# Where sums and scalings run in a hybrid decoder block: row normalisation on VectorE from PSUM, kv latent weights split earlier, gate weights scaled by ScalarE, output splits spread

## The chip, the core and the metric

The kernel runs on one core of a Trainium2 chip. The core has a matrix engine (TensorE, PE in the profile, with its weight loads as PEld), a vector engine (VectorE, DVE), a scalar engine (ScalarE, ACT), a general engine (GpSimd, POOL) and a queue for data transfers (SyncE, SP). They run in parallel, each through its own list of instructions in order, and wait for one another by semaphores. The metric is the device time of one execution in microseconds (us); of several runs the median counts.

## The reference

One decoder block on 1024 rows (S) of width 1024 (D), all in float32. What is computed:

```
h  = rmsnorm(x, mix_norm_g)
p  = h @ w_in    # q 512 | k 128 | v 128 | q latent 384 | kv latent 256 | rope key 32 | gate a 1024 | gate b 1024
A  = sliding-window attention (window 128, 8 heads on 2 kv heads, sinks, rope) of q, k, v
B  = latent attention: q from rmsnorm(q latent) @ w_uq; k, v from rmsnorm(kv latent) @ w_ukv; causal, 8 heads
y  = sigmoid(gate a) * (A @ w_o_swa) + sigmoid(gate b) * (B @ w_o_mla)
x  = x + y @ w_out
h  = rmsnorm(x, ffn_norm_g)
x  = x + (silu(h @ w_gate) * (h @ w_up)) @ w_down        # width 2816
out = rmsnorm(x, final_norm_g)
```

rmsnorm(x, g) is x times 1/sqrt(mean(x*x) + 1e-6) per row, times g per column.

## The kernel before

**Precision.** Every large product is made of three matmuls. Both factors are split into a rounded part hi and a remainder lo (function split, lines 159 to 161: ACT copies src into hi with rounding, L160, and DVE subtracts hi from src into lo, L161). mm3 (L163 to 169) then adds hi*hi, hi*lo and lo*hi in PSUM; the three lines L167, L168 and L169 are PE's rows in the profile. Weights whose rows carry the norm's gain are split by split_g: ACT scales and rounds (L215), DVE multiplies and subtracts in one instruction (L216), one piece of 128 rows at a time.

**Stages.** They follow each other on PE:

1. The q pass (about 20 to 85 us). For each of eight blocks b of 128 rows, kvq(b) makes k, v and the head half of q, q_first(b) the rest of q, from the normalised and transposed block xt[b]. square(b) sums the squares on ACT, POOL makes 1/rms and writes it on the diagonal of a 128x128 tile dg (L398; a ring of four tiles). spread(b) multiplies a matrix of ones by that tile on PE (L402), so that 1/rms stands in every partition, in PSUM (rb). normalize(b) multiplies xt[b] by it: for b < 5 (RAW) ACT copies rb to SBUF (L407) and POOL multiplies, for b = 5 to 7 DVE multiplies straight from PSUM (both L409). to_quad(b) splits xt[b] into hh and hl, h_out(b) stores it. rope_q and rope_kvq apply rope on DVE (L370 to 377) and store through SP, k_transposes and k_split bring the keys into khd.
2. The ql pass (85 to 121.5): the q latents. set_of_h(c) loads pairs of stored blocks of h back (load_set, two U buffers each) and makes sums and differences of them (t1, t2, t3, t4) for the seven-product scheme below. latent_end(b) reads the latent from PSUM. The two units of kl weights are fetched and split by st.get at b = 6 and 7.
3. The kl pass (121.5 to 156.6): the kv latents of eight blocks (lines 951 to 979), 24 matmuls each. Into it are put the first window-attention steps (sw_qT(0), sw_scores(0)), the preparation of the first gate weights (gates.prep_to, gates.mix(0)) and kv_out(b), the scaling and store of each latent.
4. The gates (156.6 to 345): class Seven (L697) makes each column j of the gates by a scheme of seven half-size products (numbered 1 to 7 and run in ORDER = 1, 6, 2, 7, 5, 4, 3). mix(j) makes three sums of weight halves on POOL (L622, L625 are the helpers sub and add), prep splits the weights of a product three products ahead, and scale_gate (L802 to 809) multiplies them by the gain, column 0 on DVE, the others on POOL, four instructions per half. Column 0 has an order written out (head). Sixteen steps of the window attention are put between the products: sw_q load, sw_qT transposes, sw_scores (DVE's max nm at L897, ACT's exponential at L905), sw_pT, sw_pv.
5. The MLA attention (345 to 548), with the stored window outputs loaded and split for the output projection near its end (load_oa, split_oa).
6. The output projections (548 to 750), then the FFN up to 1388: again class Seven for w_gate and w_up (columns of both are products g and u, prepared four ahead), then the down projection.

**What sets the order.** PE and SP run in program order up to line 1559. ACT, DVE and POOL run in program order up to the end of the kl pass (by_hand, L485 to L979); after that a planner orders these three. U is a pool of 21 buffers, V one of 17; a load or a result waits until its buffer is free. PSUM has pool ps1 (P1) and a pool of the phase (PX).

## Time and profile before

| | |
|---|---|
| median of three runs | 1392.3 us (1391.87 to 1393.46) |
| the profiled execution | 1390.31 us |
| its span, first to last instruction | 1388.5 us |
| PE busy | 1347.6 us, 97% |
| DVE, ACT, POOL busy | 922.9, 621.1, 600.9 us |
| mean granted PE clock | 0.994 of full speed |
| read from and written to HBM | 141.24 MB, 59.77 MB |

A row of the timeline reads: start in us, length in us (the summed length for several in one row, ending in x2, x4), engine, line, operation, result <- operands by their names in the program, shape, number. Brackets give the engine's idle time just before and what ended it: "[1.95 <-DVE wl L216]" is an engine that stood still for 1.95 us until the tile wl was written by DVE in line 216. A row of the groups reads: line, engine, operation, number | busy us, mean ns of one | idle time before and its releasers. A row of the waits: who waited for whom, us in total, times, the longest. PEclk is the clock that PE was granted, 1.00 being full.

### The profile page before, as it was taken

What the parts mean: (1) busy time and instruction counts of PE and PEld (TensorE: products, weight loads), DVE (VectorE), ACT (ScalarE), POOL (GpSimd) and SP (SyncE); (2) the same over time, 40 slices, a digit from 0 to 9 for tenths busy, and PEclk for the clock granted to TensorE, in tenths of its full rate; (3) what the DMA queues carried; (4) which work ended last, traced back from release to release, by engine and by line L of the source; (5) the groups of instructions that cost most, each with busy time, mean ns of one, the idle gap of its engine ahead of it and who ended that gap; (6) DMA issues with size and microseconds to landing.
All of it is one profiled execution on the core that took longest, in us unless ns stands there. A gap on an engine that the chain in (4) does not pass through costs nothing.

```text
span 1388.5 us, 18957 instructions
## 1 busy us (share of the span) xinstructions
PE 1347.6 (97%) x6600; PEld 1124.8 (81%) x6600; DVE 922.9 (66%) x1481; ACT 621.1 (45%) x1248; POOL 600.9 (43%) x643
## 2 busy tenths in 40 slices
PE   9897999999999999999999899999999999999997
PEld 6797887888888887888887688888888888888886
DVE  6868578778767788476449856655566565664762
ACT  7433455654566777553226322223233223644353
POOL 2414575766145565120021556686555652022421
PEclk9998999999999999999999999999999999999999
DMA  9454223323400010473154244454444324997504
GB/s 360 149 178 148 74 80 115 107 95 118 163 1 12 13 61 17 160 269 117 46 213 143 83 168 175 167 199 150 174 160 162 140 101 171 363 387 268 167 5 147
DMA packets 78095, 202.25 MB, mean 146 GB/s; under 512 B 8752, under 2 KB 15408, under 8 KB 78000
## 3 DMA queue, kind: packets, MB, share of 16 engines
q1 hardware_dynamic: 77856, 201.04, 40.5%
q8 instruction: 52, 0.85, 0.2%
q14 instruction: 43, 0.35, 0.1%
q10 hardware_dynamic: 144, 0.00, 0.0%
HBM read 141.24 MB, written 59.77 MB: 145 GB/s over the span
## 4 chain that ended last, share of the span: by engine, by line
PE 77%; DVE 7%; issue 4%; POOL 3%; ACT 3%; DMA 1%; SPq 0%; POOLq 0%; ACTq 0%; DVEq 0%
PE fa L169 7%; PE fa L167 7%; PE fa L168 7%; PE fb L167 5%; PE fb L168 5%; PE fb L169 5%; PE fd L169 5%; PE fd L167 5%; PE fd L168 5%; PE xo L167 2%; PE xo L169 2%; PE xo L168 2%; PE pTb L1148 2%; PE oA L167 1%; PE oA L169 1%
## 5 line engine op out<-in xcount | busy, mean ns | idle before, releaser
L161 DVE TENSOR_TENSOR wl<-wr,wl 128x512 fp32r<-128x512 f32 x150 | 153.0, 1043 | 78.7 <-ACT wl L160 78.4
L161 DVE TENSOR_TENSOR lrv<-lr,lrv 128x1024 fp32r<-128x1024 f32 x77 | 105.1, 1396 | 50.3 <-ACT lrv L160 49.2
L160 ACT CAST lrv<-lr 128x1024 fp32r<-128x1024 f32 x77 | 80.1, 1052 | 96.1 <-PE fd L169 55.8
L168 PE MATMUL fd<-lrv 128*128 128x512 f32 x308 | 119.9, 389 | 0.0
L169 PE MATMUL fd<-lrv 128*128 128x512 f32 x308 | 119.8, 389 | 0.0
L167 PE MATMUL fd<-lrv 128*128 128x512 f32 x308 | 119.8, 389 | 0.0
L622 POOL TENSOR_TENSOR wr<-wr,sm 128x512 f32<-128x512 f32 x30 | 43.6, 1452 | 122.5 <-DVE wl L161 122.5
L160 ACT CAST wl<-wr 128x512 fp32r<-128x512 f32 x150 | 87.0, 622 | 1.1 <-DVE t4l L161 0.8
L293 POOL TENSOR_SCALAR ms<-ss 128x1 f32<-128x1 f32 x32 | 8.1, 254 | 176.7 <-ACT xn L1520 111.2
L161 DVE TENSOR_TENSOR wl<-sm,wl 128x512 fp32r<-128x512 f32 x60 | 49.6, 853 | 37.3 <-ACT wl L160 37.1
L1133 POOL TENSOR_TENSOR denb<-denb,neg_one 128x1 f32<-128x1 f32 x64 | 36.5, 570 | 72.9 <-ACT p L1132 69.5
L168 PEld LDWEIGHTS fd<-lrv 128*128 128x128 f32 x308 | 57.8, 188 | 12.4 <-DVE lrv L161 0.3
L169 PEld LDWEIGHTS fd<-lrv 128*128 128x128 f32 x308 | 57.8, 188 | 12.1
L167 PEld LDWEIGHTS fd<-lrv 128*128 128x128 f32 x308 | 57.8, 188 | 11.8
L1132 ACT ACTIVATE p<-scb,nmb 128x384 f32<-128x384 f32 (+3 forms) x64 | 47.6, 744 | 35.5 <-DVE nmb L1131 34.1
L161 DVE TENSOR_TENSOR ptl<-pTb,pth 128x512 fp32r<-128x512 f32 (+2 forms) x96 | 50.1, 549 | 13.0 <-ACT pth L160 12.7
L1131 DVE CUSTOM_DVE_ANT_0 scb<-scb,mask 128x384 f32<-128x384 f32 (+3 forms) x64 | 48.4, 757 | 13.4 <-PE scb L1123 13.1
L1412 ACT ACTIVATE act<-sm 128x512 f32<-128x512 f32 x11 | 7.0, 634 | 110.6 <-DVE sm L625 110.6
L905 ACT ACTIVATE pe<-sc,nm 128x256 f32<-128x256 f32 (+1 forms) x64 | 28.8, 458 | 55.5 <-DVE nm L897 55.5
L625 POOL TENSOR_TENSOR sm<-wr,wr 128x512 f32<-128x512 f32 x30 | 40.9, 1363 | 28.4 <-DVE t4l L161 15.2
L167 PE MATMUL fb<-t3h,wl 128*128 128x512 f32 x120 | 48.0, 400 | 5.0 <-DVE pu L625 3.8
L1134 POOL TENSOR_SCALAR p<-p,denb 128x384 f32<-128x384 f32 (+3 forms) x64 | 49.1, 768 | 6.3
(347 smaller groups left out, 4370.3 us busy)
## 6 DMA issues: line engine op xcount, KB each, us to landing
lr<-la_d SPq DMA_DIRECT2D x77, 256.0 KB, 5.4
wr<-in_w_gate_dram SPq DMA_DIRECT2D x22, 512.0 KB, 3.8
wr<-in_w_up_dram SPq DMA_DIRECT2D x22, 512.0 KB, 4.9
wd<-in_w_down_dram SPq DMA_DIRECT2D x22, 512.0 KB, 7.0
rb_d<-wd SPq DMA_DIRECT2D x22, 512.0 KB, 2.6
la_d<-sd SPq DMA_DIRECT2D x22, 512.0 KB, 5.4
lr<-rb_d SPq DMA_DIRECT2D x44, 256.0 KB, 5.4
lr<-in_w_down_dram SPq DMA_DIRECT2D x33, 256.0 KB, 5.3
```

Of the source, the lines that this page charges most:

```text
L160: nc.scalar.copy(hi, src)
L161: (eng or nc.vector).tensor_tensor(lo, src, hi.bitcast(F32), op=ALU.subtract)
L167: nc.tensor.matmul(ps, ah, bh, start=first and i == 0, stop=False, skip_group_check=go_on)
L168: nc.tensor.matmul(ps, ah, bl, start=False, stop=False, skip_group_check=go_on)
L169: nc.tensor.matmul(ps, al, bh, start=False, stop=last and i == n - 1, skip_group_check=go_on)
L622: eng.tensor_tensor(out, a, b, op=ALU.subtract)
L625: eng.tensor_tensor(out, a, b, op=ALU.add)
L905: nc.scalar.activation(pe[:, h, c0:], scs[h // 2][:, h % 2, c0:], AF.Exp, scale=SC_A, bias=nm[:, h:h + 1], accum_out=den[:, h:h + 1])
L1131: nc.vector.tensor_tensor_reduce(s_, s_, m_, 1.0, -NEG, op0=ALU.add, op1=ALU.min, accum_out=nm)
L1132: nc.scalar.activation(p_, s_, AF.Exp, scale=-1.0, bias=nm, accum_out=den)
L1133: nc.gpsimd.tensor_tensor(den, den, neg_one[:, 0:1], op=ALU.pow)
L1134: nc.gpsimd.tensor_scalar(p[:, 0:w], p[:, 0:w], den, 0.0, op0=ALU.mult, op1=ALU.add)
```

## The change

It moves work between engines and along the programs of the engines, and keeps the matmuls; column 0 of the gates runs its products 2 and 6 in the other order.

- normalize always multiplies on DVE from PSUM; ACT's copy of rb and POOL's multiply go. The ring of dg has seven tiles. k_split makes both ACT copies before both subtractions. In the hand-written order of the q pass to_quad(2), to_quad(3), to_quad(6), to_quad(4), square(7) and normalize(7) come earlier, in front of rope and key steps.
- The kl weights are split at b = 0 and 2 of the ql pass. set_of_h runs latent_end ahead of its splits and POOL's subtractions in two halves. sw_q(0) is loaded at b = 6. sw_qT takes the phase's PSUM pool.
- In the kl pass mix(0) runs on DVE at i = 3, prep_to(2) at i = 4, gate part (1, 0) is loaded at i = 4; kv_out runs two blocks behind up to i = 4.
- The gates' head is gone. For j >= 1 ACT scales the gate weights, in pieces given by scale_at (product, half, first piece, count). mix runs at product 5 and no longer at 7; the sums on POOL are made in halves of 128x256.
- After the last prod_v the weights wv and wkv2 are dropped, and the window outputs are loaded and split in eight single steps of the attention.
- In the FFN mix(1) runs on DVE after the loop, with prep_to(14) ahead of it.

```diff
--- before.py
+++ after.py
...
     dgt = U("dg", F32, (P, 8, P))
-    ones, dg, rbs = dgt[:, 7], dgt[:, 0:4], dgt[:, 4:7]
+    ones, dg = dgt[:, 7], dgt[:, 0:7]
...
         rstd_of(sums.pop(b), D, r)
-        nc.gpsimd.tensor_scalar(dg[:, b % 4], ident, r, 0.0, op0=ALU.mult, op1=ALU.add)
+        nc.gpsimd.tensor_scalar(dg[:, b % 7], ident, r, 0.0, op0=ALU.mult, op1=ALU.add)
...
         rb[b] = P1("rb", (P, P))
-        nc.tensor.matmul(rb[b], ones, dg[:, b % 4], start=True, stop=True)
+        nc.tensor.matmul(rb[b], ones, dg[:, b % 7], start=True, stop=True)
...
     def normalize(b):
-        r, eng = rb.pop(b), nc.vector
-        if b < RAW:
-            nc.scalar.copy(rbs[:, b % 3], r)
-            r, eng = rbs[:, b % 3], nc.gpsimd
-        eng.tensor_tensor(xt[b], xt[b], r.unsqueeze(1).to_broadcast([P, NK, P]), op=ALU.mult)
+        nc.vector.tensor_tensor(xt[b], xt[b], rb.pop(b).unsqueeze(1).to_broadcast([P, NK, P]), op=ALU.mult)
...
         for g in range(NG):
-            split(khd[g][0][:, blk(b)], khd[g][1][:, blk(b)], pt[:, g])
+            nc.scalar.copy(khd[g][0][:, blk(b)], pt[:, g])
+        for g in range(NG):
+            sub(khd[g][1][:, blk(b)], pt[:, g], khd[g][0][:, blk(b)].bitcast(F32), nc.vector)
...
     h_out(5)
+    to_quad(2)
     rope_q(1)
-    to_quad(2)
...
     st.load_to(st.index[("ql", 0)])
+    square(7)
+    to_quad(6)
     rope_kvq(5)
-    to_quad(6)
-    square(7)
...
     h_out(6)
+    to_quad(3)
     rope_q(2)
+    normalize(7)
     k_split(4)
-    normalize(7)
-    to_quad(3)
...
     k_twice(6)
+    to_quad(4)
...
     rope_q(3)
-    to_quad(4)
...
         sub(r[:, 0], t[:, 0], r[:, 0], nc.vector)
-        sub(t[:, 0], t[:, 1], t[:, 0], nc.gpsimd)
-        split_h("t1", c, r[:, 0])
+        for k in range(0, 4, 2):
+            k = slice(k, k + 2)
+            sub(t[:, 0, k], t[:, 1, k], t[:, 0, k], nc.gpsimd)
...
         sub(t[:, 1], t[:, 1], r[:, 0], nc.vector)
-        split_h("t3", c, t[:, 0])
-        sub(t4_raw[-1][:, c % 2], r[:, 1], t[:, 1], nc.gpsimd)
-        split_h("t2", c, t[:, 1])
+        for i, src in ((1, r[:, 0]), (3, t[:, 0]), (2, t[:, 1])):
+            split_h(f"t{i}", c, src)
+        for k in range(0, 4, 2):
+            k = slice(k, k + 2)
+            sub(t4_raw[-1][:, c % 2, k], r[:, 1, k], t[:, 1, k], nc.gpsimd)
...
-        def __init__(self, pairs, ms, load, done, ahead, load_at, mix_at, head=(), at=None, scale=None):
+        def __init__(self, pairs, ms, load, done, ahead, load_at, mix_at, head=(), at=None, scale=None, scale_at=(), piece=4):
...
                 self.at.setdefault((j, load_at[1]), []).append(("load", j + 1, 1))
+                for q, *args in scale_at:
+                    self.at.setdefault((j, q), []).append(("scale", j + 1, *args))
...
             self.scale = scale
+            self.piece = piece
...
+        def scale_part(self, j, kh, k=0, n=4):
+            for k in range(k, k + n):
+                if self.scale is not None and (j, kh, k) not in self.scaled:
+                    self.scaled.add((j, kh, k))
+                    self.scale(j, kh, k, self.raws[(j, kh)])
...
             self.load_part(j, kh)
-            if self.scale is not None and (j, kh) not in self.scaled:
-                self.scaled.add((j, kh))
-                self.scale(j, kh, self.raws[(j, kh)])
+            self.scale_part(j, kh)
...
-        def mix(self, j):
+        def mix(self, j, eng=None):
...
                 s = self.sums[(j, m)] = U("sm", F32, (P, 2, 4, P))
-                add(s[:, 0], a21, a22, nc.gpsimd)
-                sub(s[:, 1], s[:, 0], a11, nc.gpsimd)
-                sub(a21, a11, a21, nc.gpsimd)
+                eng_, n = (eng, 4) if eng is not None else (nc.gpsimd, self.piece)
+                for k in range(0, 4, n):
+                    k = slice(k, k + n)
+                    add(s[:, 0, k], a21[:, k], a22[:, k], eng_)
+                    sub(s[:, 1, k], s[:, 0, k], a11[:, k], eng_)
+                    sub(a21[:, k], a11[:, k], a21[:, k], eng_)
...
             if q == 7:
-                a12 = self.part(j, m, 1, 0)
-                sub(a12, a12, self.sums[(j, m)][:, 1], nc.gpsimd)
+                a12, s1 = self.part(j, m, 1, 0), self.sums[(j, m)][:, 1]
+                for k in range(0, 4, self.piece):
+                    k = slice(k, k + self.piece)
+                    sub(a12[:, k], a12[:, k], s1[:, k], nc.gpsimd)
...
                 for what, *args in self.at.get((j, q), ()):
-                    (self.load_part if what == "load" else self.mix)(*args)
+                    {"load": self.load_part, "mix": self.mix, "scale": self.scale_part}[what](*args)
...
-    def scale_gate(j, kh, raw):
+    def scale_gate(j, kh, k, raw):
         t = raw["g"]
-        for k in range(4):
-            g = gT[:, 4 * kh + k:4 * kh + k + 1]
-            if j == 0:
-                nc.vector.tensor_scalar(t[:, k], t[:, k], g, None, op0=ALU.mult)
-            else:
-                nc.gpsimd.tensor_scalar(t[:, k], t[:, k], g, 0.0, op0=ALU.mult, op1=ALU.add)
+        g = gT[:, 4 * kh + k:4 * kh + k + 1]
+        if j == 0:
+            nc.vector.tensor_scalar(t[:, k], t[:, k], g, None, op0=ALU.mult)
+        else:
+            nc.scalar.activation(t[:, k], t[:, k], AF.Copy, scale=g)
...
-    gates = Seven(NK, "g", load_gate, gate_done, 3, (1, 6), 7, [(0, q) for q in (1, 2, 6, 7, 5, 4, 3)],
-                  {(0, 1): [("load", 1, 0)], (0, 6): [("load", 1, 1)], (0, 7): [("mix", 1)]}, scale_gate)
+    gates = Seven(NK, "g", load_gate, gate_done, 3, (1, 6), 5, scale=scale_gate, scale_at=[(2, 0, 0, 2), (7, 0, 2, 2), (7, 1, 0, 2), (5, 1, 2, 2)], piece=2)
...
             latent_end(b - 1)
-        if b >= 6:
-            wkl.append(st.get(("kl", b - 6)))
+        if b == 6:
+            sw_q(0)
+        if b in (0, 2):
+            wkl.append(st.get(("kl", b // 2)))
...
         ql_ps[b] = (t, ps, rstd_of(ss, QL))
-    sw_q(0)
...
         qn = d.pop("qn")
-        ptq = P1("qT", (P, 2, P))
+        ptq = PX("qT", (P, 2, P))
...
         if i == 3:
-            gates.prep_to(2)
+            gates.mix(0, nc.vector)
...
             sw_scores(0)
+            gates.prep_to(2)
...
             t4_of_h(i - 4)
-        if i == 5:
-            gates.mix(0)
         scaled.append((t, r, b))
-        if i >= 1:
+        if i == 4:
+            gates.load_part(1, 0)
+        while len(scaled) > (2 if i < 5 else 1):
             kv_out(*scaled.pop(0))
-    kv_out(*scaled.pop(0))
+    while scaled:
+        kv_out(*scaled.pop(0))
     gates.prep_to(3)
+    gates.load_part(1, 0)
...
         prod_v(b)
+    del wv
+    wkv2.pop()
...
-    def load_oa(sh):
-        for g in range(2):
-            oa_raw[(g, sh)] = U("oar", F32, (P, 2, 512))
-            nc.sync.dma_start(oa_raw[(g, sh)], oa_d[2 * g + sh])
-    def split_oa(g, sh):
-        raw = oa_raw.pop((g, sh))
-        hi, lo = halves_of((P, 2, 512), True)
-        for c in range(2):
-            split(hi[:, c], lo[:, c], raw[:, c])
-            oaT[(2 * g + c, sh)] = (hi[:, c], lo[:, c])
+    def load_oa(g, sh):
+        oa_raw[(g, sh)] = U("oar", F32, (P, 2, 512)), halves_of((P, 2, 512), True)
+        nc.sync.dma_start(oa_raw[(g, sh)][0], oa_d[2 * g + sh])
+    def split_oa(g, sh, c):
+        raw, (hi, lo) = oa_raw[(g, sh)] if c == 0 else oa_raw.pop((g, sh))
+        split(hi[:, c], lo[:, c], raw[:, c])
+        oaT[(2 * g + c, sh)] = (hi[:, c], lo[:, c])
...
     wo = {}
+    OA_LOAD = {-26: (0, 0), -22: (1, 0), -14: (0, 1), -10: (1, 1)}
+    OA_SPLIT = {-22: (0, 0, 0), -20: (0, 0, 1), -18: (1, 0, 0), -16: (1, 0, 1),
+                -10: (0, 1, 0), -8: (0, 1, 1), -6: (1, 1, 0), -4: (1, 1, 1)}
...
         e = t - (NT - 8)
-        if e == -13:
-            load_oa(0)
-        if e == -10:
-            load_oa(1)
-        if e in (-10, -9, -7, -6):
-            i = (-10, -9, -7, -6).index(e)
-            split_oa(i % 2, i // 2)
+        if e in OA_LOAD:
+            load_oa(*OA_LOAD[e])
+        if e in OA_SPLIT:
+            split_oa(*OA_SPLIT[e])
...
             ffn.prep_to(12)
-        if i == 5:
-            ffn.mix(1)
...
             late_split(i - 2)
+    ffn.prep_to(14)
+    ffn.mix(1, nc.vector)
...
```

More of the change, by code (lines that the diff above doesn't have):

```diff
@@ L169, in mm3, with sub, add @@
             nc.tensor.matmul(ps, al, bh, start=False, stop=last and i == n - 1, skip_group_check=go_on)
+    def sub(out, a, b, eng):
+        eng.tensor_tensor(out, a, b, op=ALU.subtract)
+    def add(out, a, b, eng):
+        eng.tensor_tensor(out, a, b, op=ALU.add)
     def blk(b, n=1):
@@ L618, in hybrid_block_kernel @@
     del wqa
-    def sub(out, a, b, eng):
-        eng.tensor_tensor(out, a, b, op=ALU.subtract)
-    def add(out, a, b, eng):
-        eng.tensor_tensor(out, a, b, op=ALU.add)
     hq = {}
```

## The prediction

> **What bounds the kernel now.** I read the page's shares first, then busy time by stretch, then each row of PE's timeline that begins with an idle time, then the VectorE (DVE), ScalarE (ACT) and GpSimd (POOL) rows under it.
>
> ```profile
> span 1388.5 us, 18957 instructions
> PE 1347.6 (97%) x6600; PEld 1124.8 (81%) x6600; DVE 922.9 (66%) x1481; ACT 621.1 (45%) x1248; POOL 600.9 (43%) x643
> ```
>
> PE is the bound: 1388.5 - 1347.6 = 40.9 us is all its idle time. The matmuls stay the same in number and shape, so only this idle time, and matmuls run at a lowered clock, can be won. By stretch (time, length, PE, its weight loads, DVE, ACT, POOL, granted PE clock, DMA share, GB/s):
>
> ```profile
> 20.00:85.00 65.00, 60.95 (x364) 52.49 (x363) 54.72 (x115) 31.36 (x80) 22.15 (x23) 1.00 0.56 195
> 85.00:121.50 36.50, 36.50 (x196) 36.12 (x195) 23.00 (x53) 10.93 (x28) 13.88 (x18) 1.00 0.58 197
> 121.50:156.60 35.10, 27.23 (x203) 26.45 (x203) 22.03 (x61) 15.45 (x49) 14.04 (x26) 0.85 0.23 77
> 156.60:190.00 33.40, 29.12 (x143) 23.45 (x142) 24.37 (x49) 16.25 (x44) 22.94 (x32) 1.00 0.35 111
> 190.00:345.00 155.00, 152.70 (x774) 126.14 (x773) 122.30 (x279) 83.19 (x235) 101.18 (x150) 1.00 0.31 104
> 512.00:548.00 36.00, 32.49 (x199) 27.07 (x199) 33.64 (x66) 28.46 (x64) 19.91 (x26) 1.00 0.13 45
> 750.00:786.00 36.00, 31.00 (x128) 23.75 (x127) 31.18 (x39) 17.71 (x32) 14.75 (x10) 0.95 0.20 70
> 786.00:1380.00 594.00, 594.00 (x2621) 491.64 (x2620) 357.60 (x393) 204.96 (x315) 274.71 (x202) 1.00 0.51 182
> ```
>
> The rows are the q pass, the ql pass, the kl pass, the start of the gates, the rest of the gates, the end of the MLA attention, the start of the FFN, and all that follows it. Idle PE in them: 4.05, 0, 7.87, 4.28, 2.30, 3.51, 5.00 and 0. The change edits the first seven; they hold 27.0 of the 40.9, and two have a clock below 1.
>
> **Part 1, the q pass: normalise 0 to 4 on DVE from PSUM, later rope, K copies before K subtractions.**
>
> ```profile
> 43.76 3.49 DVE L161 TENSOR_TENSOR hl<-xt,hh 128x512 fp32r<-128x512 f32 x2
> 44.07 2.62 POOL L409 TENSOR_TENSOR xt<-xt,dg 128x1024 f32<-128x1024 f32 x1 [2.40 <-ACT dg L407]
> 48.45 0.49 PE L402 MATMUL rb<-dg 128*128 128x128 f32 x2 [1.76 <-POOL dg L398]
> 51.15 1.28 DVE L161 TENSOR_TENSOR hl<-xt,hh 128x512 fp32r<-128x512 f32 x2
> 56.84 0.50 PE L169 MATMUL kvq<-wv,hl 128*128 128x512 f32 x1 [0.64 <-DVE hl L161]
> 58.32 2.48 DVE L377 TENSOR_TENSOR qn<-rp 128x128 f32<-128x128 f32 x1
> 64.29 0.39 PE L169 MATMUL qa<-wv,hl 128*128 128x256 f32 x1 [1.03 <-DVE hl L161]
> L409 DVE TENSOR_TENSOR xt<-xt,rb x3: 1210/1210/1212, 41.4 to 62.4; 128x1024 f32<-128x1024 f32 x3
> ```
>
> The two hl subtractions that begin at 43.76, beside the POOL multiply of 2.62, take 3.49; the same two at 51.15, with no multiply beside them, take 1.28. At 58.32 a 128x128 rope addition takes 2.48, though a subtraction four times as wide takes 0.64. So a POOL multiply holds DVE up by some 2 us (2.21 and at least 1.84), while the same multiply done by DVE from PSUM costs 1.21 (the last row, b = 5 to 7). Added: five multiplies, 5 x 1.21 = 6.05 us of DVE. Removed: five POOL multiplies and the five ACT copies of the broadcast. If all five held DVE up by 2, DVE gains 4 us; if only the two shown did, it loses 2. I take a small gain, since the three PE stalls name the tiles that come late through this: hl twice, and once POOL's dg, for which POOL first had to end its multiply. Their sum is 3.43; with two short ones the stretch idles 4.05. The rope additions pushed back have k_twice and the q store on SP behind them; the next K transposes come a whole block of PE work later, and that covers them. The K copies of ACT in front of both subtractions cost nothing as long as PE has that block; without it, one copy. The larger dg ring lets the squares run ahead. I take **3.8 won**, ends 1.5 (the DVE loss of 2 lands on PE) and 4.05.
>
> [...]
>
> **Part 2, the kl weights: split in the ql pass at b = 0 and 2, not 6 and 7.**
>
> ```profile
> 123.75 0.39 PE L168 MATMUL kl<-wl,hh 128*128 128x256 f32 x1 [1.95 <-DVE wl L216]
> 130.32 0.58 PE L167 MATMUL kl<-wh,hh 128*128 128x256 f32 x1 [4.88 <-ACT wh L215]
> 131.41 1.66 DVE L216 SCALAR_TENSOR_TENSOR wl<-wr,gT,wh 128x256 fp32r<-128x256 f32 x4
> 131.93 0.58 PE L168 MATMUL kl<-wl,hh 128*128 128x256 f32 x1 [1.04 <-DVE wl L216]
> 132.00:135.00 3.00, 3.00 (x14) 3.00 (x15) 2.32 (x9) 0.31 (x1) 0.98 (x2) 0.50 0.00 0
> 137.00:145.00 8.00, 8.00 (x69) 8.00 (x68) 3.64 (x12) 2.65 (x8) 1.48 (x4) 1.00 0.06 19
> L215 ACT ACTIVATE wh<-wr,gT 128x256 fp32r<-128x256 f32 x8 | 3.4, 499 | 0.0
> 97.11 0.69 DVE L622 TENSOR_TENSOR hr<-ht,hr 128x512 f32<-128x512 f32 x1 [5.92 <-DMA ht<-h_d]
> ```
>
> The three PE waits are 1.95 + 4.88 + 1.04 = 7.87, all for these splits, and all the idle time of the stretch. After the 4.88 the clock is 0.50 and 14 matmuls take 3.00 (0.214 each); later 69 take 8.00 (0.116). At 0.116 the 203 matmuls of the stretch need 23.5 us; with the few longer ones of the window attention I estimate 24.2, so 27.23 - 24.2 = 3.0 goes with the clock. Gone together: **10.9**. The splits are two units of four ACT (the group: 3.4 us for eight) and four DVE pieces (1.66 each unit): 3.4 and 3.3 us moved into the ql pass, where ACT is busy 10.93 and DVE 23.00 of 36.5. That slack hides them; without it 3.3 would fall on PE. Their loads were issued long before, and SP issues no more for them. New here: they hold two more U buffers through the pass, and the loads of the h sets need U buffers. DVE waited 5.92 at 97.11 for such a load. Also sw_q(0)'s load goes on SP in front of the last latent stores: one small issue, nothing that PE waits for. The ends are 10.9 - 5.92 = 5.0, and 10.9. The sums of set_of_h are reordered with latent_end ahead of the splits and POOL's subtractions halved: same work, PSUM of ql released earlier; the stretch has no PE idle to win, and one more POOL start per half to lose, nothing while the next consumer, the gates, is 30 us off.
>
> **Part 3, the head of the gates: mix(0) by DVE in the kl pass, gate load earlier.**
>
> ```profile
> 155.37 1.29 POOL L625 TENSOR_TENSOR sm<-wr,wr 128x512 f32<-128x512 f32 x1
> 159.75 1.74 POOL L622 TENSOR_TENSOR wr<-wr,sm 128x512 f32<-128x512 f32 x1
> 155.46 1.74 DVE L161 TENSOR_TENSOR t4l<-h,t4h 128x512 fp32r<-128x512 f32 x1 [1.56 <-ACT t4h L160]
> 165.23 0.39 PE L889 MATMUL sc<-khd,qs 128*128 128x256 f32 x1 [2.01 <-DVE qs L873]
> ```
>
> From 155.37 to 161.5 POOL adds up weight halves (four operations, first and last shown) while DVE's t4l takes 1.74 instead of 0.64; DVE arrives late and PE waits 2.01 for qs at 165.23, the largest of 4.28 idle in this stretch. With the three sums on DVE at i = 3 (3 x 0.69, the price of hr at 97.11: 2.1 us) they lie ahead of the gates. DVE's work in the kl pass is then 22.03 - 3.3 (Part 2) + 2.1 = 20.8 against 24.2 of PE. Product 6 of column 0 now comes second and needs these sums: if they are late, their 2.1 fall on PE. What they delay is the prep_to(2) and the scores behind them on DVE. The load of gate (1,0) now stands on SP in front of kv stores; nobody waits for those within this stage. I take **3.4 won**, ends 1.4 (the 2.0 comes back a little earlier in the kl pass) and 4.3.
>
> **Part 4, the rest of the gates: scaling on ACT, POOL's sums halved, mix at q = 5.**
>
> ```profile
> L809 POOL TENSOR_SCALAR wr<-wr,gT 128x256 f32<-128x256 f32 x56 | 30.3, 559 | 6.3 <-DMA wr<-in_w_gt_dram 6.3
> ACT pe L905 <- DVE nm L897: 55.5, 16, 4.6
> ```
>
> POOL loses 56 instructions of 0.559, 30.3 us. ACT gets 56 of about 0.499 (the 128x256 scaled copies of Part 2), 27.9 us, in groups of two, four and two per gate column; ACT's order is strict, so what stands behind a group of four (2.0 us) are casts for PE and exponentials. ACT has 155 - 83.19 = 72 us free there, of which 55.5 over the whole stage is spent waiting for nm before the exponentials, 3.5 each. That covers a group of four if it falls there; if the cover goes, each piece costs PE 0.5. POOL's sums in halves are twice as many starts; POOL, with 30.3 less to do, has room for them, and DVE gets in between. PE idles 2.30 now. I take **0.2 lost**; ends 2 won (nearly all of that 2.30) and 6 lost (two pieces, 1.0, in the open in six of the seven columns); more than that is rival C.
>
> **Part 5, the MLA end: output splits spread over 18 steps.**
>
> ```profile
> 515.84 2.38 DVE L161 TENSOR_TENSOR wv<-oar,wv 128x512 fp32r<-128x512 f32 x2
> ```
>
> Eight splits (1.2 of DVE each in this row) came two at a time within four steps; DVE is busy 33.64 of 36.00 there, PE idles 3.51. One at a time over 18 steps removes the clumps, but DVE has the same work and the earlier steps get it. I take **1.0 won**; ends 1 lost and 2.5 won. The buffers come from dropping weights no longer used; the loads on SP are the same four, earlier.
>
> **Part 6, the FFN head: mix(1) by DVE after the loop.**
>
> ```profile
> 763.00 1.29 DVE L161 TENSOR_TENSOR wl<-sm,wl 128x512 fp32r<-128x512 f32 x2
> 776.50 3.42 DVE L161 TENSOR_TENSOR wl<-sm,wl 128x512 fp32r<-128x512 f32 x2
> 767.56 1.68 POOL L625 TENSOR_TENSOR sm<-wr,wr 128x512 f32<-128x512 f32 x1 [15.21 <-DVE t4l L161]
> 773.95 0.47 PE L167 MATMUL fb<-t3h,wl 128*128 128x512 f32 x1 [0.84 <-ACT wl L160]
> 780.67 0.47 PE L167 MATMUL fb<-t3h,wl 128*128 128x512 f32 x1 [3.75 <-DVE pu L625]
> 785.09 0.40 PE L167 MATMUL fa<-t1h,wl 128*128 128x512 f32 x1
> ```
>
> Six sums and two subtractions of 1.7 follow each other on POOL from 767.56; under them a pair of DVE splits takes 3.42 instead of 1.29, and PE waits 0.84 and 3.75. The 12 matmuls from 780.67 to 785.09 take 4.42; at the pitch of the last stretch above, 594.00 / 2621 = 0.227, twelve need 2.7, so 1.7 goes with the clock. DVE gets six sums, 6 x 0.64 = 3.9 us, after the loop, ahead of the adds for the next products: covered by prepared weights (prep_to(14) goes first). Uncovered, 3.9 come back. I take 0.84 + 3.75 + 1.7 = **6.3 won**, ends 2.4 and 6.7 (all 5.00 idle and the clock).
>
> **The sum.** 3.8 + 10.9 + 3.4 - 0.2 + 1.0 + 6.3 = 25.2, less 0.9 for new short waits (an estimate: one or two like the 0.64 and 0.84 above): 24.3. The profiled execution took 1390.31, 2.0 below the median of 1392.3; so it would be 1366.0, and the median **1368.0**. All upper ends together: 4.05 + 10.9 + 4.3 + 2 + 2.5 + 6.7 = 30.5, 1361.8. All lower ends: 1.5 + 5.0 + 1.4 - 6 - 1 + 2.4 = 3.3, 1389; they have different causes and would hardly meet.
>
> **Rivals.**
>
> A. The forecast: the holes close, 1363 to 1373. For it: each wait names a tile that the edit makes earlier.
>
> B. DVE or the U buffers become the bound of the kl pass. Once PE no longer stalls there, DVE's 20.8 stand against 24.2 of PE, with kv outputs and scores in its order, and two buffers are held longer. One more load wait like the 5.92, or DVE late by as much, gives 5 to 10 back: 1373 to 1378. Against it: the ql pass has 13 us of DVE slack.
>
> C. Slower: ACT's scaling stands in front of casts that PE needs. 56 x 0.499 = 27.9 exposed, plus POOL's 6.3 wait for the gate load, now ACT's: 1392.3 - 24.3 + 34.2 = 1402. It decides from 0.43 us per piece on (24.3 / 56). Against it: 72 us of ACT idle in the stretch.
>
> D. The sums moved to DVE win nothing, because DVE takes as long as it waited before. Parts 1, 3 and 6 hold 3.8 + 3.4 + 6.3 = 13.5; without them 1381.5. For it, 6.05, 2.1 and 3.9 are added to DVE, busy 54.72 of 65 and 31.18 of 36. Against it: the lengthenings of 2 us and more in the rows above exceed these. [...]
>
> **How the numbers follow.** A 0.70, B 0.18, D 0.05, C 0.05, and 0.02 that gains and losses cancel. The range goes from 1362 to 1379, A and B, and leaves out D, C and the tails. What a measurement can tell from no change is 0.2%, 2.8 us; slower holds C, 0.05, same 0.02, faster the rest, 0.93.
>
> **What would show it.** In the changed kernel PE should have no idle above 1 us in the q pass, the kl pass should last 24 to 26 us at clock 1.00, with no wait for wh or wl of L216; hl pairs should take 1.28 throughout; the FFN head should lose the 3.75 and its low clock. Wrong would be: a long wait of DVE for ht, PE waiting for casts behind gate scaling, or a stall above 3 us anywhere new, with a lowered clock behind it.

## The result, and the profile after

The changed kernel takes 1360.43 us (median of four runs, 1359.93 to 1361.71) against 1392.19 for the kernel before in the same comparison: ratio 0.9772, 95% interval 0.9755 to 0.9789. The forecast was 1368.0, with a range from 1362 to 1379: the direction was right, the time lies 1.6 us below the range, and even below the 1361.8 of all upper ends together. The profiled execution took 1360.20, 30.1 less than the one profiled before.

The page of the changed kernel:

```profile
span 1358.4 us, 18987 instructions
PE 1338.1 (99%) x6600; PEld 1121.8 (83%) x6600; DVE 913.4 (67%) x1495; ACT 641.5 (47%) x1299; POOL 557.7 (41%) x610
```

PE's idle time went from 40.9 to 1358.4 - 1338.1 = 20.3 us, that is by 20.6, but the span shrank by 30.1. PE's busy time also shrank, by 9.5 us, with the same 6600 matmuls. Matched matmul by matmul with the changed kernel, the stretches of lowered clock in the kernel before cost 2.6 in the kl pass and 1.6 in the FFN, 4.2 in all; the rest is what the forecast missed.

To compare stages, I cut both traces at the same matmuls: the first kvq product with split weights, the first ql, kl and gate products, the first transpose of latents, the first output product, the second FFN product (748.78; the first begins at 743.22), the first down product. Before (columns as in the prediction's first table):

```profile
13.30:85.01 71.71, 67.66 (x393) 57.86 (x391) 58.80 (x124) 36.23 (x89) 24.38 (x29) 1.00 0.60 215
...
121.52:156.62 35.10, 27.23 (x203) 26.46 (x202) 22.05 (x61) 15.43 (x49) 14.04 (x26) 0.85 0.23 77
156.62:349.07 192.45, 185.87 (x933) 152.88 (x931) 148.03 (x330) 100.03 (x279) 125.39 (x182) 1.00 0.32 106
349.07:546.96 197.89, 190.77 (x1145) 162.47 (x1144) 154.76 (x307) 136.03 (x300) 96.16 (x130) 1.00 0.13 44
...
748.78:1171.35 422.57, 417.56 (x1834) 343.83 (x1832) 269.76 (x329) 132.94 (x238) 235.96 (x165) 1.00 0.42 153
```

and after:

```profile
13.37:78.66 65.29, 65.29 (x392) 57.65 (x391) 56.03 (x127) 34.46 (x82) 10.63 (x24) 1.00 0.64 232
...
115.17:139.30 24.13, 24.13 (x203) 24.13 (x202) 19.40 (x55) 12.49 (x41) 13.69 (x25) 1.00 0.42 140
139.30:326.20 186.90, 183.92 (x932) 153.07 (x931) 137.10 (x332) 122.86 (x337) 100.38 (x156) 1.00 0.33 109
326.20:524.10 197.90, 190.75 (x1146) 162.74 (x1144) 155.24 (x307) 135.55 (x300) 95.95 (x130) 1.00 0.13 44
...
725.91:1141.75 415.84, 415.39 (x1833) 342.86 (x1832) 272.82 (x335) 132.85 (x238) 230.38 (x159) 1.00 0.43 155
```

| stage | forecast, us won | measured | idle PE that went |
|---|---|---|---|
| q pass | 3.8 | 6.42 | 4.05 |
| ql pass | 0 | 0 | 0 |
| kl pass | 10.9 | 10.97 | 7.87 |
| gates | 3.4 - 0.2 | 5.55 | 3.60 |
| MLA attention | 1.0 | -0.01 | -0.03 |
| output projections | 0 | 0.01 | 0.03 |
| FFN products | 6.3 | 6.73 | 4.56 |
| reserve for new waits | -0.9 | | |
| sum | 24.3 | 29.7 | 20.1 |

The missing 0.4 of 30.1 is the down projection (0.5 won) less the first loads (0.1 lost). Every stage that won, won more than its idle time. The largest waits that the change left in the gates are two of one kind, 80 us apart:

```profile
198.68 0.50 PE L167 MATMUL fa<-hh,wl 128*128 128x512 f32 x1 [1.27 <-ACT pu L797]
...
278.47 0.50 PE L167 MATMUL fa<-hh,wl 128*128 128x512 f32 x1 [1.27 <-ACT pu L797]
```

### The profile page after: what moved, and what is told of

It is laid out like the page before. It is cut to its first block, busy times and chain, and to the rows that moved or that the text cites. A ratio compares the mean times of both kernels' runs of the same rounds, so it can differ in the third digit from the quotient of the medians.

```text
span 1358.4 us, 18987 instructions
## 1 busy us (share of the span) xinstructions
PE 1338.1 (99%) x6600; PEld 1121.8 (83%) x6600; DVE 913.4 (67%) x1495; ACT 641.5 (47%) x1299; POOL 557.7 (41%) x610
## 4 chain that ended last, share of the span: by engine, by line
PE 83%; DVE 6%; POOL 3%; issue 3%; ACT 3%; DMA 1%; SPq 0%; POOLq 0%; ACTq 0%; DVEq 0%
PE fa L169 7%; PE fa L167 7%; PE fa L168 7%; PE fb L169 6%; PE fb L167 6%; PE fb L168 6%; PE fd L168 5%; PE fd L167 5%; PE fd L169 5%; PE xo L168 2%; PE xo L169 2%; PE xo L167 2%; PE pTb L1166 2%; PE oA L167 1%; PE oA L169 1%
## 5 line engine op out<-in xcount | busy, mean ns | idle before, releaser
L161 DVE TENSOR_TENSOR wl<-wr,wl 128x512 fp32r<-128x512 f32 x150 | 150.0, 1024 | 72.2 <-ACT wl L160 71.8
L172 POOL TENSOR_TENSOR wr<-wr,sm 128x512 f32<-128x512 f32 (+1 forms) x38 | 46.3, 1228 | 152.2 <-DVE wl L161 118.7
L168 PEld LDWEIGHTS fd<-lrv 128*128 128x128 f32 x308 | 57.8, 188 | 11.8
L160 ACT CAST pth<-pTb 128x512 fp32r<-128x512 f32 (+2 forms) x96 | 42.9, 482 | 13.4 <-PE pTb L1166 12.9
L167 PE MATMUL fb<-t2h,wl 128*128 128x512 f32 x120 | 47.4, 395 | 0.0
```

The lines of the kernel that those rows point to most:

```text
L160: nc.scalar.copy(hi, src)
L161: (eng or nc.vector).tensor_tensor(lo, src, hi.bitcast(F32), op=ALU.subtract)
L167: nc.tensor.matmul(ps, ah, bh, start=first and i == 0, stop=False, skip_group_check=go_on)
L168: nc.tensor.matmul(ps, ah, bl, start=False, stop=False, skip_group_check=go_on)
L172: eng.tensor_tensor(out, a, b, op=ALU.subtract)
```

## The experiments

Each kernel is the changed one with one thing altered. The single runs are read by the length of their stages, cut as above, since the start differs between executions: the first gate product began at 139.30 to 139.85 in the traces of the changed kernel (two), of the scaling on POOL and of the two versions at the end. Stages differ too: with the same code for the stage, the kl pass took 24.13 to 25.05 in the traces here, the gates 186.19 to 187.35 and the MLA attention 197.05 to 198.21, and a difference within that shows nothing. Three runs of the kernel before beside them took 1389.04, 1388.86 and 1389.74.

### What a stall costs: the FFN with weights one product ahead

```diff
-    ffn.n_ahead = 4
+    ffn.n_ahead = 1
```

> The changed kernel with the FFN's weights prepared one product ahead and not four, so that many products begin with a wait of PE. It measures what a stall costs. Theory 2: the time from the first FFN product to the first down product grows by PE's marked idle time and some 0.3 us more per stall. Rival: it grows by the idle time alone, within a tenth of it. Matmuls at a lowered clock are counted by themselves.

In this run the first down matmul stands ten matmuls earlier, so the stage is cut by the number of its matmuls. It took 501.5 us, 85.7 more than the changed kernel's 415.84.

```profile
726.57:1228.06 501.49, 445.39 (x1833) 345.10 (x1832) 295.49 (x335) 132.78 (x238) 235.99 (x159) 0.98 0.37 129
```

Marked idle time is 56.1, 55.7 more than in the changed kernel. Set against the matmuls of the changed kernel, pair by pair, the seven stretches of halved clock cost 11.8. That leaves 85.7 - 55.7 - 11.8 = 18.2 us, with 40 new marked stalls: 0.46 each, more than the 0.3 expected. The rival (idle time alone, within a tenth) falls. How it comes about is seen in the one stall of the kernel before at 64.29, beside the same kind of product without a stall in the changed kernel:

```profile
64.29 0.39 PE L169 MATMUL qa<-wv,hl 128*128 128x256 f32 x1 [1.03 <-DVE hl L161]
64.51 0.28 PE L167 MATMUL qa<-wv,hh 128*128 128x256 f32 x1
```

```profile
58.04 0.28 PE L167 MATMUL qa<-wv,hh 128*128 128x256 f32 x1
58.16 0.28 PE L168 MATMUL qa<-wv,hh 128*128 128x256 f32 x1
58.27 0.28 PE L169 MATMUL qa<-wv,hl 128*128 128x256 f32 x1
```

A row is 0.28 long, but rows begin 0.12 apart: 0.16 us of each lies under the next one. In a stall that 0.16 is counted as busy, and the row after the stall begins 0.22 and not 0.12 after it: 0.10 more. So this stall cost its marked idle time and about 0.26, and between rows like these a delay under 0.16 is not marked at all. In the q pass eight stalls over 0.05 us had 4.03 of idle and took 5.33 with the 0.16 in front; the slower restarts behind them and delays that are not marked took 1.12; the rest cancels: 6.4. The 0.46 of this run is higher because many of its delays are of the unmarked kind: 93 pairs of matmuls without a marked stall between them, the restarts behind its stalls among them, were further apart by 10.5 us in all.

### The q pass: engine or order

Three kernels. The first puts normalise 0 to 4 back on POOL, keeping the new order; with ACT's copies in the tile, the ring of dg has four tiles again:

```diff
-    ones, dg = dgt[:, 7], dgt[:, 0:7]
+    ones, dg, rbs = dgt[:, 7], dgt[:, 0:4], dgt[:, 4:7]
...
-        nc.vector.tensor_tensor(xt[b], xt[b], rb.pop(b).unsqueeze(1).to_broadcast([P, NK, P]), op=ALU.mult)
+        r, eng = rb.pop(b), nc.vector
+        if b < RAW:
+            nc.scalar.copy(rbs[:, b % 3], r)
+            r, eng = rbs[:, b % 3], nc.gpsimd
+        eng.tensor_tensor(xt[b], xt[b], r.unsqueeze(1).to_broadcast([P, NK, P]), op=ALU.mult)
```

> The changed kernel with one part undone: rows 0 to 4 are again normalised by POOL from ACT's copy of the broadcast (the ring of dg has four tiles again); the new order of the q pass stays. Theory 1: POOL's multiply holds up the DVE instructions beside it; hl pairs take 3 us and more again, PE stalls return and the q pass (first kvq to first ql matmul, 65.3 us in the changed kernel, 71.7 before) grows by 3 to 6 us. Rival: the new order alone closed the stalls; it grows by less than 1. Theory 2, on the missing 2.4 us: a PE stall costs its marked idle time and about 0.3 us of lost overlap of matmuls, so the stage grows by idle + 0.3 per stall. Rival to theory 2: it grows by just the idle time.

The q pass took 67.29, 2.00 more than the changed kernel. DVE's pair of 3.49 is back as it was, and PE does not wait for it. The only wait is for dg:

```profile
42.52 3.49 DVE L161 TENSOR_TENSOR hl<-xt,hh 128x512 fp32r<-128x512 f32 x2
...
42.83 2.63 POOL L415 TENSOR_TENSOR xt<-xt,dg 128x1024 f32<-128x1024 f32 x1 [2.39 <-ACT dg L413]
...
45.55 0.51 POOL L299 TENSOR_SCALAR ms<-ss 128x1 f32<-128x1 f32 x1
...
47.22 0.49 PE L408 MATMUL rb<-dg 128*128 128x128 f32 x2 [1.77 <-POOL dg L404]
```

The small instructions for 1/rms stand behind the 2.63 us multiply in POOL's queue: ms begins at 45.55, when the multiply ends, and dg follows without a pause, so the smaller ring is not what it waits for. Neither expectation on the size holds: it is more than 1 and less than 3. The one on the cost of a stall does: 1.77 marked cost 2.00.

The second kernel keeps the multiply on DVE but reads ACT's copy in SBUF (nc.vector in the place of nc.gpsimd above, the ring of four too):

> The changed kernel, with rows 0 to 4 normalised by DVE, but from ACT's copy in SBUF, so with two inputs in SBUF (the ring of dg has four tiles). Theory 1a: only POOL's long multiply did harm, whichever source DVE uses; the q pass stays within 0.7 us of 65.3 us. Rival 1b: the PSUM source is what matters, since DVE with two SBUF inputs is held up by what POOL still does there; the 1.21 us multiplies get longer and the q pass grows by more than 1 us.

```profile
L415 DVE TENSOR_TENSOR xt<-xt,dg x5: 1215/1218/1226, 27.1 to 62.2; 128x1024 f32<-128x1024 f32 x5
...
L415 DVE TENSOR_TENSOR xt<-xt,rb x3: 1214/1214/1214, 40.0 to 59.1; 128x1024 f32<-128x1024 f32 x3
...
43.52 1.22 DVE L415 TENSOR_TENSOR xt<-xt,dg 128x1024 f32<-128x1024 f32 x1
...
43.93 0.85 POOL L299 TENSOR_SCALAR ms<-ss 128x1 f32<-128x1 f32 x1 [3.70 <-ACT x L401]
...
45.94 0.49 PE L408 MATMUL rb<-dg 128*128 128x128 f32 x2 [0.70 <-POOL dg L404]
```

and in the changed kernel at the same place:

```profile
43.30 1.22 DVE L411 TENSOR_TENSOR xt<-xt,rb 128x1024 f32<-128x1024 f32 x1
...
43.56 0.19 POOL L299 TENSOR_SCALAR ms<-ss 128x1 f32<-128x1 f32 x1 [3.54 <-ACT x L401]
```

With two inputs in SBUF a multiply of DVE takes 1.218, with PSUM 1.214: DVE is not slowed, with POOL's long work gone. The pass took 66.34, 1.05 more, above the bound of 0.7 that 1a had given itself and by another cause than 1b: one wait of 0.70 for dg. POOL is slowed here: ms takes 0.85 and ends with the multiply that reads SBUF, against 0.19 beside the one that reads PSUM. That is 0.66 of the lateness of dg; behind ACT's copy the square begins 0.37 later, but what stands before the copy is 0.21 later too. So the source does matter, through POOL's small instruction, in this one place.

The third keeps DVE and the seven dg tiles, and restores the old order and the paired K split (two of the moved places shown):

```diff
-    to_quad(2)
     rope_q(1)
+    to_quad(2)
...
-    square(7)
-    to_quad(6)
     rope_kvq(5)
+    to_quad(6)
+    square(7)
```

> The changed kernel with the old order of the q pass (to_quad behind rope, square(7) and normalize(7) late, K copies and subtractions in turn), but rows 0 to 4 still normalised by DVE from PSUM and the ring of seven dg tiles. With POOL's multiply back and the new order the q pass had grown by 2.0 us of the 6.4 won, by one wait for dg that stood behind the multiply in POOL's queue. Theory: order and engine each close stalls of their own, so the old order brings back the 4.4 us of the waits for hl and those near 40 us, and no wait for dg. Rival: the two overlap, either closes the waits for hl, and the q pass grows by 2 us or less.

The pass took 70.10: 4.8 more. No wait for dg, and the waits for hh and hl are back:

```profile
40.45 0.39 PE L167 MATMUL qa<-wv,hh 128*128 128x256 f32 x1 [0.24 <-ACT hh L160]
...
55.97 0.50 PE L169 MATMUL kvq<-wv,hl 128*128 128x512 f32 x1 [1.30 <-DVE hl L161]
...
63.42 0.38 PE L169 MATMUL qa<-wv,hl 128*128 128x256 f32 x1 [1.03 <-DVE hl L161]
```

4.8 and 2.0 together make 6.8, near the 6.4 won: the two edits close separate stalls. In this kernel no multiply of POOL is beside DVE, and PE waits 1.03 for the same hl as before and 1.30 for the one that it waited 0.64 for. So those waits did not come from DVE being held up by it. Which of the moves closes which wait was not tried.

### The kl weights split late

```diff
-        if b in (0, 2):
-            wkl.append(st.get(("kl", b // 2)))
+        if b >= 6:
+            wkl.append(st.get(("kl", b - 6)))
```

> The changed kernel with the kl weights split at b = 6 and 7 of the ql pass again. Theory: the kl pass (first kl matmul to first gate product, 24.1 us in the changed kernel, 35.1 before) grows by 9 to 11 us, with three waits for L215 and L216 of some 8 us and a halved clock after the long one; total 1369 to 1372. Rival: other edits (set_of_h's order, latent_end ahead) bring half of it, and the pass grows by 3 to 6 only.

1368.83. The kl pass took 33.45, 9.3 more, with the waits expected, and the clock halved for 6.8 us from 121.86 on:

```profile
116.49 0.39 PE L168 MATMUL kl<-wl,hh 128*128 128x256 f32 x1 [0.94 <-DVE wl L222]
...
121.71 0.47 PE L167 MATMUL kl<-wh,hh 128*128 128x256 f32 x1 [3.52 <-ACT wh L221]
...
123.92 0.58 PE L168 MATMUL kl<-wl,hh 128*128 128x256 f32 x1 [1.75 <-DVE wl L222]
```

The total lies just under the 1369 to 1372 expected. The step is right as it was put; 1.7 us of the 10.97 are not given back, since the three waits add up to 6.21 here and to 7.87 in the kernel before. Which other edit shortened them was not tried.

### The first gate sums on POOL

```diff
-            gates.mix(0, nc.vector)
+            gates.mix(0)
```

> The changed kernel with mix(0) at the same place, i = 3 of the kl pass, but on POOL, in pieces of 128x256. Theory: POOL's sums hold DVE up there and a stall of 1 to 4 us comes at the start of the gates or in the kl pass. Rival: the earlier place was enough, and the time stays within 0.5 us of 1360.4.

1359.62; the kl pass 24.13 as in the changed kernel, the gates 187.05 against 186.90. The rival holds: on POOL at i = 3 the sums do no harm that shows.

### The gate weights scaled on POOL

```diff
-            nc.scalar.activation(t[:, k], t[:, k], AF.Copy, scale=g)
+            nc.gpsimd.tensor_scalar(t[:, k], t[:, k], g, 0.0, op0=ALU.mult, op1=ALU.add)
```

> The changed kernel with the gate weights of columns 1 to 7 scaled on POOL again, at the new places and with the sums at the new place. Theory: POOL, with 56 more instructions in front of its sums, delivers them later, and the gates (first gate product to first latent transpose, 186.9 us in the changed kernel, 192.45 before) grow by 1 to 5 us. Rival: ACT's scaling is what makes pu late (the two waits of 1.27 us); the gates shrink by 2 to 3. Third: no difference beyond 0.5, since both engines have room.

1363.82; the gates took 190.61, 3.7 more. The two waits for pu stay (1.31 and 1.30); one wait for qs comes back, and the clock is halved behind it, which together make the 3.7. The size is that of the theory, but the wait is for a 1/rms and not for the sums:

```profile
141.24 2.52 POOL L822 TENSOR_SCALAR wr<-wr,gT 128x256 f32<-128x256 f32 x4
...
144.72 0.48 DVE L960 SCALAR_TENSOR_TENSOR lat<-lat,rstd,lg 128x256 f32<-128x256 f32 x1 [1.68 <-POOL rstd L302]
...
147.51 0.38 PE L902 MATMUL sc<-khd,qs 128*128 128x256 f32 x1 [2.26 <-DVE qs L886]
```

This is the stall of the kernel before at 165.23, with another cause in front: POOL has bulk work (there mix(0), here the scaling) ahead of the tiny 1/rms of the last kv latents, DVE waits for that rstd in order, and the casts of qs stand behind it on DVE. The kernel before shows the same wait in its row at 162.44:

```profile
162.44 0.48 DVE L947 SCALAR_TENSOR_TENSOR lat<-lat,rstd,lg 128x256 f32<-128x256 f32 x1 [2.10 <-POOL rstd L296]
```

### The output splits in clumps

```diff
-        if e in OA_SPLIT:
-            split_oa(*OA_SPLIT[e])
+        if e in (-10, -9, -7, -6):
+            i = (-10, -9, -7, -6).index(e)
+            split_oa(i % 2, i // 2)
```

(and the loads at -13 and -10 again)

> The changed kernel with the window outputs loaded and split in clumps again. Theory: the MLA attention (197.9 us both before and in the changed kernel) has its waits from the softmax chain and not from these splits; it stays within 0.3 us. Rival: the spread splits win 1 us and something else in the change loses it there; it grows by about 1.

The MLA attention took 197.87 against 197.90: no difference, as expected. In twelve traces with spread splits it took 197.05 to 198.21; in five of them one wait of some 0.76 for ob, near 71 or 114 us into the stage, is missing, with the same code. The waits are for the softmax chain (POOL p, ACT p, DVE ob and ptl) in all of them, but not for the same links. With the splits in clumps, here and in the kernel before, PE waits twice for ob near them, 0.36 and 0.51. In all twelve traces with spread splits both are gone, and two waits for ptl of 0.35 to 0.6, which the others lack, stand in their place, with others a little longer. So the spreading did close the waits of the clumps, and opened about as much elsewhere.

### The FFN's sums on POOL

```diff
-    ffn.prep_to(14)
-    ffn.mix(1, nc.vector)
...
+        if i == 5:
+            ffn.mix(1)
```

> The changed kernel with the FFN's mix(1) on POOL in the loop at i = 5 again. Theory: the 6.7 us of this stage come back whole (422.6 against 415.8 from the first FFN product to the first down product), with DVE's pairs of splits at 3.4 us, a wait above 3 us and a halved clock for 3.4 us. Rival: with the earlier edits in place, less than 3 come back.

1367.30; the stage took 422.53, all 6.7 back, as the theory had it:

```profile
754.03 3.42 DVE L161 TENSOR_TENSOR wl<-sm,wl 128x512 fp32r<-128x512 f32 x2
...
758.20 0.77 PE L167 MATMUL fb<-t3h,wl 128*128 128x512 f32 x1 [3.73 <-DVE pu L175]
```

Here DVE's lengthening beside POOL's sums (3.42 for the pair, as before, where the pair at 763.00 took 1.29) is what PE waits for, as the prediction had it: the 0.68 us addition that makes pu stands behind the lengthened splits on a DVE that had no idle time since 743.7.

### Two versions meant to be faster

The two waits of 1.27 for pu: ACT, whose copy of pu they wait for, has stood still for a sum of POOL before; and POOL has stood still between two halves of the same sum (changed kernel, ACT and POOL):

```profile
190.84 0.62 ACT L160 CAST wl<-sm 128x512 fp32r<-128x512 f32 x1 [3.81 <-POOL sm L172]
...
195.61 0.47 ACT L918 ACTIVATE pe<-sc,nm 128x256 f32<-128x256 f32 x1 [3.66 <-DVE nm L910]
...
198.03 0.60 ACT L797 COPY pu<-fa 128x512 f32<-128x512 f32 x1
```

```profile
177.57 0.74 POOL L175 TENSOR_TENSOR sm<-wr,wr 128x256 f32<-128x256 f32 x1 [0.96 <-ACT wr L822]
...
184.13 0.20 POOL L920 TENSOR_TENSOR den<-den,es 128x4 f32<-128x4 f32 x1 [5.82 <-ACT pe L918]
```

The planner put the window attention's den, which waits 5.82 us for exponentials, between the sums of one column. One version gives the sums to DVE, the other gives out their first half one product earlier, at product 7:

```diff
-                self.at.setdefault((j, mix_at), []).append(("mix", j + 1))
+                self.at.setdefault((j, mix_at), []).append(("mix", j + 1) + ((nc.vector,) if scale_at else ()))
```

```diff
+                if scale_at:
+                    self.at[(j, 7)].append(("half", j + 1))
                 self.at.setdefault((j, mix_at), []).append(("mix", j + 1))
...
```

In the second, "half" makes the three sums for k 0 and 1, and mix then begins at k = 2. The changed kernel was taken again beside them.

> The changed kernel again, on the same chip as the two versions beside it: 1359 to 1362 us.

> The changed kernel with the sums of gate columns 1 to 7 on DVE and not on POOL. In the changed kernel POOL's sums stand behind the window attention's den, ACT waits 3.8 us for them twice, and PE waits 1.27 us for pu twice (3 us with what the stalls cost besides). Theory: these waits go, 1357 to 1358. Rival: 7 x 3 x 0.69 = 14.5 us more of DVE make nm and the splits late; 1361 or more.

> The changed kernel with the first half of each gate column's sums (k 0 and 1) given out one product earlier, at product 7, still on POOL. Theory: the sums then pass POOL ahead of den, the two waits of 1.27 us go, 1357 to 1358. Rival: the order that the planner picks puts them behind den all the same, no change within 0.7 us of the changed kernel.

| kernel | median us | lowest to highest | ratio to before, 95% interval |
|---|---|---|---|
| changed kernel | 1360.88 | 1359.68 to 1361.98 | 0.9787, 0.9774 to 0.9800 |
| sums on DVE | 1361.50 | 1360.56 to 1362.10 | 0.9791, 0.9778 to 0.9804 |
| half of the sums earlier | 1356.84 | 1355.97 to 1357.02 | 0.9757, 0.9744 to 0.9770 |

On DVE the two waits go, but others take their place (0.76 for a cast of weights, 0.25 to 0.38 three times for qs), and the gates take 187.78; in time it is no different from the changed kernel, as its rival had it. With half of the sums earlier, all six instructions pass POOL ahead of den, and the gates take 183.02: 3.9 us less, for two marked waits of 1.27 and the smaller delays around them. One wait of 0.52 is left. This version beats both kernels, at the lower edge of the 1357 to 1358 expected; its runs and those of the changed kernel beside it do not overlap.

```profile
178.55 0.74 POOL L175 TENSOR_TENSOR sm<-wr,wr 128x256 f32<-128x256 f32 x1 [0.96 <-ACT wr L840]
...
182.28 0.74 POOL L172 TENSOR_TENSOR wr<-wr 128x256 f32<-128x256 f32 x1
...
185.23 0.20 POOL L938 TENSOR_TENSOR den<-den,es 128x4 f32<-128x4 f32 x1 [2.22 <-ACT pe L936]
```

## Why the prediction was wrong

The result is 7.6 us below the forecast: 5.4 in the stages (29.7 against 24.3), 0.4 outside them, and 1.8 in the step from the profiled execution to the median.

**The step that failed first** is in the prediction's second paragraph: "only this idle time, and matmuls run at a lowered clock, can be won". The stall at 64.29 also cost the 0.16 us of a matmul that no longer lay under the next, and about 0.10 at the restart. This part was put at nothing; with the delays too short to be marked it was 2.4 in the q pass, 2.0 in the gates and 0.4 in the FFN, 4.8 of the 5.4. It put the upper end of the q pass too low (4.05, measured 6.42) and, by a hair, that of the FFN (6.7, measured 6.73). In the kl pass it did no harm, since the estimate there was made from the pitch of undisturbed matmuls (203 x 0.116 and some longer ones, 24.2; measured 24.13). The changed kernel ran the q pass without a marked stall: costed by pitch, its upper end would have been 6.4.

**Part 1, the q pass.** Forecast 3.8 with upper end 4.05, measured 6.42. The size failed by the step above, and the mechanism for the most part: I put the waits down to POOL's multiply holding DVE up. With that multiply back and DVE's 3.49 with it, PE waited for dg alone, 2.0 us; with the old order back and no multiply on POOL, the waits for hh and hl cost 4.8. The order of the q pass (to_quad behind rope, square and normalise late, the paired K split) was the main cause. What I had right is that dg stood behind the multiply in POOL's queue. The traces do show the lengthening (3.49 beside the multiply, 1.28 without), but it was not what PE waited for. The three normalises of 1210 to 1212 ns from PSUM had no bulk work of POOL beside them, so they did not test whether the source matters; ms with 0.85 and 0.19 beside the two sources does, from POOL's side.

**Part 2, the kl pass.** Right: 10.9 forecast, 10.97 measured, and splitting late again gives 9.3 of it back. DVE's 5.92 wait for a load, which bounded it from below, is there as before (at 92.11), but no second one came, and PE has no idle time in the ql pass and in the kl pass.

**Parts 3 and 4, the gates.** Forecast 3.2 together, measured 5.55. I attributed the 2.01 wait for qs to DVE's t4l being stretched by mix(0). DVE's row of 2.10 shows that it waited for the tiny rstd behind POOL's sums, and the run with scaling on POOL made the same stall with no mix(0) there at all. So the earlier place of mix(0) was what counted; moving it to DVE as well was not needed (187.05 with it on POOL at i = 3, within the scatter of this stage). Part 4's sign was wrong: ACT's scaling, which I took to lose 0.2, saves 3.7 against POOL's at the same places, by keeping POOL's queue free. The halved sums on POOL brought a wait of their own, den in the midst of a sum, two stalls of 1.27; I had costed them at nothing. Which edits closed the other waits of the gates (the longest 1.33, the rest 0.53 and less) was not tried.

**Part 5, the MLA end.** Forecast 1.0, measured 0, within its ends. Of the idle time of the stretch, 0.87 was the clumps' and went, near to the 1.0; that the waits would come back at other links of the softmax chain was put at nothing.

**Part 6, the FFN head.** Forecast 6.3, measured 6.73, and the whole comes back with POOL's sums. Its 3.9 us of new DVE work stayed hidden, as expected. The 0.4 above is what its two stalls cost besides their idle time.

**The level.** I added 2.0 for the median over the profiled execution. That offset belonged to the runs of one comparison: for the changed kernel it was 0.2 (1360.43 against 1360.20), and nine runs of the kernel before beside the last versions had a median of 1390.63, 0.3 above its profiled execution. The 2.0 moved the forecast away from the result, and without it all upper ends together, 30.5, would not have been passed by the 30.1 of the profiled executions.

Rivals B, C and D did not come. In one place that the change leaves alone, what D feared is so: moving the gates' other sums to DVE wins nothing (1361.50).

## What to carry to other kernels

Cost a PE stage by the pitch of undisturbed matmuls times their number, not by its idle time: the stall at 64.29 cost about 0.26 us more than its marked idle time, the wait for dg with POOL's normalise 0.23, each of the 40 in the FFN with weights one ahead 0.46 on average, and delays under 0.16 between rows 0.28 long were not marked. Before blaming an engine that runs slowly, ask which tile PE waits for and what stood in front of it in that engine's queue; tiny reductions behind bulk work on the same in-order engine caused the waits for dg (1.76 and 1.77) and for qs (2.01 and 2.26) here, and the rows that show it are the waits of the engine between. When bulk work is cut in pieces, look where a planner puts a waiting instruction between the pieces.

## What the runs showed of the hardware

**The clock.** PE's clock was halved behind some stalls of 2 us and not behind others: behind the 2.01 at 836.68 in the FFN with weights one ahead, not behind the 2.01 at 165.23 in the kernel before. In the traces it is switched on a grid of 3.41 us: in the kernel before the clock is 0.50 from 126.20 to 136.43 (10.23) and from 781.55 to 784.96 (3.41), and the 645.12 at full clock between them are 189 steps of 3.413; with the kl weights split late it was halved for 6.8. A stretch of one such step, with PE's busy time and the clock granted in it, and then the next step, in the kernel before, in the FFN with weights one ahead (twice), and with POOL's normalise back:

```profile
122.78:126.19 3.41, 1.69 (x11) 1.49 (x11) 2.65 (x10) 0.62 (x1) 0.92 (x2) 1.00 0.55 154
126.19:129.60 3.41, 0.00 (x0) 0.00 (x0) 3.34 (x9) 0.98 (x2) 0.95 (x2) 0.50 0.88 310
```

```profile
833.95:837.36 3.41, 1.40 (x7) 0.71 (x5) 1.39 (x2) 1.87 (x4) 3.25 (x4) 1.00 0.46 185
837.36:840.77 3.41, 3.41 (x10) 2.54 (x10) 3.41 (x3) 1.87 (x4) 3.33 (x3) 0.50 0.75 202
977.31:980.72 3.41, 1.77 (x7) 1.22 (x8) 2.15 (x3) 2.96 (x6) 3.33 (x3) 1.00 0.56 229
980.72:984.13 3.41, 3.41 (x17) 2.80 (x16) 3.41 (x3) 0.78 (x2) 3.33 (x3) 1.00 0.97 288
```

```profile
43.82:47.23 3.41, 1.64 (x9) 1.01 (x7) 3.38 (x4) 0.56 (x4) 3.07 (x4) 1.00 0.96 370
47.23:50.64 3.41, 3.41 (x17) 2.83 (x18) 3.03 (x9) 2.04 (x6) 0.00 (x0) 1.00 0.07 24
```

Three more steps at full clock: in the kernel before, the one from 778.14 had 0.88 us busy and was followed by half clock, the one from 163.74 had 1.87 and was not; with the gate weights scaled on POOL, the one from 144.44 had 1.15 and was followed by half clock. So steps with 0.88, 1.15, 1.40 and 1.69 busy of 3.41 lost the clock, and those with 1.64, 1.77 and 1.87 did not: about half a step idle was enough, with no exact bound to be read. In the two stalls of 2.01 it depended on where they fell on the grid: the one at 165.23 lay across two steps, with 2.89 and 1.87 busy, and did not lose the clock; the one at 836.68 lay in a single step, with 1.40, and did. In the FFN with weights one ahead, a halved step cost 11.8 / 7 = 1.7 us.
